# A differential-attention block on one Trainium2 core: GpSimd combines the two softmax maps, and the head's output is scaled only in its norm

## The chip, the core and the metric

The program runs on one core of one Trainium2 chip. The metric is the device time of one execution in microseconds (us). The kernel before takes 1281.97 us, the median of three runs (1281.35 to 1283.07). The engines are named as in the profile: PE is TensorE (matmuls and transposes, with PEld for its weight loads), DVE is VectorE, ACT is ScalarE, POOL is GpSimd and SP is SyncE, which issues most of the DMAs. Each engine works through its own instructions in a fixed order, and a semaphore holds an instruction until what it needs is there.

## The reference

The block is one decoder layer on 1024 tokens of width 1024, in float32. After an RMS norm one projection gives a pooling branch, queries, keys and values, and two gates. What the change touches is the differential attention: four heads, each with two maps of head dimension 64 and a value of width 128.

```python
def probs(qq, kk):
    s = jnp.einsum('bhqd,bhkd->bhqk', qq, kk).astype(jnp.float32) * scale + bias
    s = jnp.where(causal, s, -jnp.inf)
    return jax.nn.softmax(s, axis=-1)

a = probs(qa, k1) - lam * probs(qb, k2)
o = jnp.einsum('bhqk,bhkd->bhqd', a.astype(vh.dtype), vh)
...
o = rms_norm(o, subln_g) * (1.0 - lambda_init)     # per head, over the 128 value columns
```

`rms_norm` divides by the root of the mean square plus 1e-6. Then both branches go through their own projections, are multiplied by their gates, summed, projected, normed and added to the input, and a SwiGLU feed-forward part of hidden width 2816 follows.

## The kernel before

The program has a projection part (units of seven products that save an eighth one, about 0 to 338 us), the attention (about 338 to 500 us), the second branch projection and the output projection, and the feed-forward part. Matrix products are done in pieces: each float32 operand is split by ACT into a rounded high part and by DVE into the remainder, and three matmuls of 512 columns replace one.

The attention works on 32 steps, one for each head h and each block qb of 128 queries. With E = exp(scores), a step needs L = 128 (qb + 1) columns. `scores(h, qb)` makes for each of the two maps m: matmuls into a PSUM pair (L734, L735), one DVE instruction that adds the distance bias, leaves the negated scores in the tile E[m] and their minimum in nm (L738), and one ACT exponential that also sums each row (L741). Then three DVE instructions join the two maps: the reciprocals of both sums, the factor cf = sum0 * nlam / sum1 where nlam is minus lambda, and E0 + cf * E1 (L745 to L747). So the joined map is still too large by the first map's sum. `transposes(h, qb)` turns it on PE in blocks of 128 (L762), and ACT and DVE split it into AT (L764). `values(h, qb)` multiplies by V (L776), and ACT and DVE scale the two halves of the product by 1/sum0 and add them into O (L781, L782); ACT sums the squares (L784). `head_norm(h)` makes one factor per row from these sums (DVE, then a power on POOL, L126) and DVE multiplies the head's O by it (L795); `turn_head` transposes O for the projection (L808 to L811).

The steps of the first three heads go in the order 7, 0, 6, 1, 5, 2, 4, 3 of qb, those of the last in falling order. The code issues the scores of step i + 4, then the transposes of step i + 1, then the values of step i. Between these, `filling()` hands out matmuls of the rest of the last projection unit and of the branch projection `branch(0, ...)` as filler for PE, at a pace given by PACES. Outside the stretches marked as manual, a planner with its own costs then sets the final order on every engine, so a change of an instruction's engine also moves others. `branch(1, ...)` follows the attention in the code; its first two products need only the later half of the queries.

The tiles E and AT share 14 buffers (tag b4) with others, the small columns 20 (tag small); the PSUM has two buffers each for pairs, for mm (transposes and values) and for fil (filler).

Of the kernel before, what the change touches and what calls it, by code (L numbers as in the profile page):

```python
# [39 lines left out]
def block_kernel(ctx, tc, x, w_in, pool_mix, pool_scale, w_branch_a, lam_q1, lam_k1, lam_q2,  # L40
# [72 lines left out]
    make_identity(nc, ident)  # L113
    mhalf = cp.tile([P, 8], F32, name="mhalf")
    nc.vector.memset(mhalf, -0.5)
    junk = cp.tile([P, D], mybir.dt.bfloat16, name="junk")
    psc = cp.tile([P, 4], F32, name="psc")
    sgc = cp.tile([P, 1], F32, name="sgc")
# [596 lines left out]
    def scores(h, qb):  # L715

        QA, QB, K, V = heads[h]
        slope = 0.25 ** (h + 1)
        L = P * (qb + 1)
        nj = 1 if L <= HALF else 2  # L720
        w = L // nj
        q = slice(qb * P, (qb + 1) * P)
        if nj == 1:
            E = b4([P, 2, HALF], F32, "E")
            E = [E[:, 0, :L], E[:, 1, :L]]
        else:
            E = [b4([P, S], F32, "E")[:, :L] for _ in range(2)]
        nm, sums = small(2, "nm"), small(2, "sums")
        dv = negd[:, S - L:S].rearrange("p (j w) -> p j w", j=nj)
        for m in range(2):  # L730
            sc = pair("s")
            for j in range(nj):
                c = slice(j * w, (j + 1) * w)
                nc.tensor.matmul(sc[:, j, :w], QA[:, m, q], K[:, m, c], start=True, stop=False)  # L734
                nc.tensor.matmul(sc[:, j, :w], QB[:, m, q], K[:, m, c], start=False, stop=True)  # L735
            e = E[m].rearrange("p (j w) -> p j w", j=nj)

            nc.vector.tensor_tensor_reduce(out=e, in0=sc[:, :nj, :w], in1=dv, scale=-slope,  # L738
                                           scalar=3.0e38, op0=ALU.add, op1=ALU.min,
                                           accum_out=nm[:, m:m + 1])  # L740
            nc.scalar.activation(E[m], E[m], AF.Exp, bias=nm[:, m:m + 1], scale=-1.0,  # L741
                                 accum_out=sums[:, m:m + 1])
            yield
        rec, cf = small(2, "rec"), small(1, "cf")
        nc.vector.reciprocal(rec, sums)  # L745
        nc.vector.tensor_scalar(cf, sums[:, 0:1], rec[:, 1:2], nlam, op0=ALU.mult, op1=ALU.mult)
        nc.vector.scalar_tensor_tensor(out=E[0], in0=E[1], scalar=cf, in1=E[0], op0=ALU.mult, op1=ALU.add)  # L747
        attends[h, qb] = E[0], rec
        yield

    O = [b4([P, NB, P], F32, "O") for _ in range(NH)]
    oss = [cp.tile([P, NB], F32, name=name("oss")) for _ in range(NH)]

    def transposes(h, qb):
        E, rec = attends[h, qb]
        ats = []
        for b0 in range(0, qb + 1, 4):
            n = min(4, qb + 1 - b0)
# [6 lines left out]
            sub(AT[:, 1, :n * P], pt[:, :n * P], AT[:, 0, :n * P])  # L765
            ats.append(AT)
            yield
        attends[h, qb] = ats, rec

    def values(h, qb):  # L770
        V = heads[h][3]
        ats, rec = attends[h, qb]
        o = mm("o")[:, :2 * P]
        for b in range(qb + 1):
            for j in range(2):
# [2 lines left out]
            if b == 3:  # L778
                yield
        ov = O[h][:, qb, :]  # L780
        nc.scalar.mul(ov, o[:, P:], rec[:, 0:1])  # L781
        nc.vector.scalar_tensor_tensor(out=ov, in0=o[:, :P], scalar=rec[:, 0:1], in1=ov,  # L782
                                       op0=ALU.mult, op1=ALU.add)
        sumsq(ov, oss[h][:, qb:qb + 1])  # L784
        yield

# [1 line left out]

    def head_norm(h, b=slice(0, NB)):
        n = b.stop - b.start  # L790
        r = rstd_of(oss[h][:, b], n, P)

        def scale():
            o = O[h][:, b, :]
            nc.vector.tensor_tensor(out=o, in0=o, in1=r.unsqueeze(2).to_broadcast([P, n, P]), op=ALU.mult)  # L795

        if h < NH - 1:
            defer(LAG, scale)
        else:
            scale()  # L800
# [480 lines left out]
```

## Time and profile before

| | |
|---|---|
| median of three runs | 1281.97 us (1281.35 to 1283.07) |
| the profiled execution's own time | 1280.2 us |
| its span in the trace | 1278.3 us |
| PE, DVE, ACT, POOL busy, share of the span | 97%, 66%, 46%, 10% |
| granted PE clock, mean | 0.999 |
| attention, about | 338 to 500 us |

The span runs from the first to the last instruction of the trace; 1.9 us of the profiled execution's time lie around it. Shares of the whole span average over stages with different limits, so the attention is read by stretches. PE's busy time holds instructions that overlap: a matmul of 512 columns is shown with some 390 ns, while in a stretch without gaps one starts every 222 ns (90 in 20 us). A busy PE can therefore hold gaps that its busy time does not show.

### The profile page before, as it was taken

The page shows a single profiled execution, that of the slowest core. Times are in us where ns is not written, and L with a number is a line of the kernel's source. Part 1 is how long each engine was busy: PE and PEld are TensorE (multiplying, and loading weights), DVE is VectorE, ACT ScalarE, POOL GpSimd, SP SyncE. Part 2 cuts the span into 40 slices and gives each one's busy share as a digit, 9 for nine tenths or more (in the row PEclk, how much of TensorE's full clock was granted, in tenths as well). Part 3 has the DMA queues.
Part 4 walks back from the last instruction along what each step waited for, and adds up shares of the span by engine and source line. Part 5 has one row for each costly group of instructions (what it writes and reads, how often), then busy time and mean ns, then how long its engine had stood idle before and what let it go on. Part 6 is the DMA issues. An engine that isn't in the chain of part 4 may idle for free.

```text
span 1278.3 us, 15840 instructions
## 1 busy us (share of the span) xinstructions
PE 1246.2 (97%) x5952; PEld 1039.0 (81%) x5952; DVE 839.4 (66%) x1307; ACT 583.0 (46%) x1037; POOL 129.5 (10%) x113
## 2 busy tenths in 40 slices
PE   6999999999989999999999999999999999999997
PEld 6988778888778887878878888888888888888886
DVE  6885775534479987755599556456556537965666
ACT  7453344434586764245454333333333334454542
POOL 1000000000101100000102110111111111000221
PEclk9999999999999999999999999999999999999999
DMA  8263346323788312634224233233322368733235
GB/s 279 83 202 117 134 151 216 110 89 107 251 246 222 121 51 76 196 133 156 98 68 140 99 103 95 93 106 124 108 99 91 107 207 293 250 91 98 87 106 205
DMA packets 139788, 179.16 MB, mean 140 GB/s; under 512 B 8000, under 2 KB 94528, under 8 KB 137280
## 3 DMA queue, kind: packets, MB, share of 16 engines
q1 hardware_dynamic: 127776, 146.56, 36.6%
q10 hardware_dynamic: 11936, 31.60, 6.3%
q8 instruction: 46, 0.75, 0.3%
q14 instruction: 30, 0.25, 0.1%
HBM read 124.39 MB, written 53.74 MB: 139 GB/s over the span
## 4 chain that ended last, share of the span: by engine, by line
PE 79%; DVE 7%; ACT 5%; DMA 4%; issue 4%; POOL 1%; ACTq 0%; SPq 0%; DVEq 0%; POOLq 0%
PE Y L241 9%; PE Y L242 9%; PE Y L243 9%; PE X L241 5%; PE X L242 5%; PE X L243 5%; PE Yd L242 3%; PE Yd L243 3%; PE Yd L241 3%; PE Z L242 2%; PE Z L243 2%; PE Z L241 2%; PE o L776 2%; PE wo L934 2%; PE wo L935 2%
## 5 line engine op out<-in xcount | busy, mean ns | idle before, releaser
L162 DVE TENSOR_TENSOR p<-Z,p 128x512 f32<-128x512 f32 x35 | 24.2, 691 | 156.5 <-PE Z L243 156.4
L242 PE MATMUL Y<-A_lo,Wh 128*128 128x512 f32 x296 | 115.7, 391 | 0.3 <-DVE A_lo L87 0.3
L241 PE MATMUL Y<-A_hi,Wh 128*128 128x512 f32 x296 | 115.3, 389 | 0.0
L243 PE MATMUL Y<-A_hi,Wl 128*128 128x512 f32 x296 | 115.2, 389 | 0.0
L241 PE MATMUL Y<-S_hi,Wh 128*128 128x512 f32 x280 | 109.3, 390 | 0.0
L241 PE MATMUL X<-S_hi,Wh 128*128 128x512 f32 x280 | 109.1, 390 | 0.1
L242 PE MATMUL Y<-S_lo,Wh 128*128 128x512 f32 x280 | 109.2, 390 | 0.0
L243 PE MATMUL Y<-S_hi,Wl 128*128 128x512 f32 x280 | 109.1, 390 | 0.0
L243 PE MATMUL X<-S_hi,Wl 128*128 128x512 f32 x280 | 109.0, 389 | 0.0
L242 PE MATMUL X<-S_lo,Wh 128*128 128x512 f32 x280 | 109.0, 389 | 0.0
L202 ACT CAST Wh<-wf_t 128x1024 fp32r<-128x1024 f32 x70 | 72.8, 1053 | 66.9 <-PE X L242 30.4
L87 DVE TENSOR_TENSOR w_op<-wd,w_op 128x512 fp32r<-128x512 f32 x77 | 56.0, 728 | 52.9 <-ACT w_op L166 52.9
L202 ACT CAST Wh<-w_raw 128x1024 fp32r<-128x1024 f32 x72 | 60.6, 843 | 62.4 <-PE Z L242 40.0
L87 DVE TENSOR_TENSOR Wl<-wf_t,Wh 128x1024 fp32r<-128x1024 f32 x70 | 86.5, 1243 | 1.3 <-ACT Wh L202 1.3
L166 ACT CAST w_op<-wd 128x512 fp32r<-128x512 f32 x77 | 47.9, 623 | 79.5 <-PE Yd L243 31.9
L87 DVE TENSOR_TENSOR Wl<-w_raw,Wh 128x1024 fp32r<-128x1024 f32 x72 | 69.4, 964 | 14.7 <-ACT Wh L202 14.7
L242 PE MATMUL Yd<-w_op,s_op 128*128 128x512 f32 x176 | 68.7, 390 | 0.3 <-DVE w_op L87 0.2
L241 PE MATMUL Yd<-w_op,s_op 128*128 128x512 f32 x176 | 68.6, 390 | 0.0
L243 PE MATMUL Yd<-w_op,s_op 128*128 128x512 f32 x176 | 68.3, 389 | 0.0
L162 DVE TENSOR_TENSOR wf_t<-w_raw,wf_t 128x512 f32<-128x512 f32 x70 | 65.6, 938 | 1.0
L242 PEld LDWEIGHTS Y<-A_lo,Wh 128*128 128x128 f32 x296 | 55.6, 188 | 12.0 <-DVE A_lo L87 0.7
L241 PEld LDWEIGHTS Y<-A_hi,Wh 128*128 128x128 f32 x296 | 55.6, 188 | 11.6
(263 smaller groups left out, 3054.5 us busy)
## 6 DMA issues: line engine op xcount, KB each, us to landing
s_raw<-fsd SPq DMA_DIRECT2D x35, 512.0 KB, 3.7
w_raw<-in_w_in_dram SPq DMA_DIRECT2D x32, 512.0 KB, 4.0
w_raw<-in_w_ffn_gate_dram SPq DMA_DIRECT2D x22, 512.0 KB, 3.7
w_raw<-in_w_ffn_up_dram SPq DMA_DIRECT2D x22, 512.0 KB, 3.7
fsd<-fss SPq DMA_DIRECT2D x11, 1024.0 KB, 3.8
wd<-in_w_ffn_down_dram SPq DMA_DIRECT2D x44, 256.0 KB, 5.0
fsd<-F SPq DMA_DIRECT2D x33, 256.0 KB, 2.3
qkd<-qk_st ACTq DMA_DIRECT2D x16, 512.0 KB, 3.7
```

Source lines behind the costliest of these rows:

```text
L87: nc.vector.tensor_tensor(out=o, in0=a, in1=f32(hi), op=ALU.subtract)
L162: nc.vector.tensor_tensor(out=o, in0=a, in1=b, op=op)
L166: nc.scalar.copy(hi, a)
L202: nc.scalar.copy(hi, a)
L241: nc.tensor.matmul(o, ah, bh, start=start, stop=False, skip_group_check=goes_on)
L242: nc.tensor.matmul(o, ah, bl, start=False, stop=False, skip_group_check=goes_on)
L243: nc.tensor.matmul(o, al, bh, start=False, stop=stop, skip_group_check=goes_on)
L776: nc.tensor.matmul(o, ats[b // 4][:, j, b % 4 * P:(b % 4 + 1) * P], V[:, b, :, :], start=b == 0 and j == 0, stop=b == qb and j == 1)
L934: nc.tensor.matmul(o[e], mh[:, k, :], wl, start=False, stop=False)
L935: nc.tensor.matmul(o[e], ml[:, k, :], wh, start=False, stop=k == KD - 1)
```

## The change

Four things are changed.

1. The three joining instructions leave DVE. POOL now makes cf = sum0 * nlam (one column), rec = sum1 to the power -1 (one column, with a constant tile `mone`), multiplies E1 by rec and cf (two per-partition scalars in one instruction), and adds E1 to E0.
2. 1/sum0 is no longer made. ACT copies one half of the value product and DVE adds the other to it, so O stays larger by sum0.
3. The sums of a head are kept in a tile `esum` of their own until the head's norm, and EPS is multiplied by the square of sum0 there. This takes two DVE instructions in place of one in `head_norm`.
4. The constant tile `mone` is set once on DVE.

```diff
--- before.py
+++ after.py
@@ -113,6 +113,8 @@
     make_identity(nc, ident)
     mhalf = cp.tile([P, 8], F32, name="mhalf")
     nc.vector.memset(mhalf, -0.5)
+    mone = cp.tile([P, 1], F32, name="mone")
+    nc.vector.memset(mone, -1.0)
     junk = cp.tile([P, D], mybir.dt.bfloat16, name="junk")
     psc = cp.tile([P, 4], F32, name="psc")
     sgc = cp.tile([P, 1], F32, name="sgc")
@@ -725,7 +727,7 @@
             E = [E[:, 0, :L], E[:, 1, :L]]
         else:
             E = [b4([P, S], F32, "E")[:, :L] for _ in range(2)]
-        nm, sums = small(2, "nm"), small(2, "sums")
+        nm, sums = small(2, "nm"), esum[h][:, qb, :]
         dv = negd[:, S - L:S].rearrange("p (j w) -> p j w", j=nj)
         for m in range(2):
             sc = pair("s")
@@ -741,18 +743,20 @@
             nc.scalar.activation(E[m], E[m], AF.Exp, bias=nm[:, m:m + 1], scale=-1.0,
                                  accum_out=sums[:, m:m + 1])
             yield
-        rec, cf = small(2, "rec"), small(1, "cf")
-        nc.vector.reciprocal(rec, sums)
-        nc.vector.tensor_scalar(cf, sums[:, 0:1], rec[:, 1:2], nlam, op0=ALU.mult, op1=ALU.mult)
-        nc.vector.scalar_tensor_tensor(out=E[0], in0=E[1], scalar=cf, in1=E[0], op0=ALU.mult, op1=ALU.add)
-        attends[h, qb] = E[0], rec
+        cf, rec = small(1, "cf"), small(1, "rec")
+        nc.gpsimd.tensor_tensor(out=cf, in0=sums[:, 0:1], in1=nlam, op=ALU.mult)
+        nc.gpsimd.tensor_tensor(out=rec, in0=sums[:, 1:2], in1=mone, op=ALU.pow)
+        nc.gpsimd.tensor_scalar(E[1], E[1], rec, cf, op0=ALU.mult, op1=ALU.mult)
+        nc.gpsimd.tensor_tensor(out=E[0], in0=E[0], in1=E[1], op=ALU.add)
+        attends[h, qb] = E[0]
         yield
 
+    esum = [cp.tile([P, NB, 2], F32, name=name("esum")) for _ in range(NH)]
     O = [b4([P, NB, P], F32, "O") for _ in range(NH)]
     oss = [cp.tile([P, NB], F32, name=name("oss")) for _ in range(NH)]
 
     def transposes(h, qb):
-        E, rec = attends[h, qb]
+        E = attends[h, qb]
         ats = []
         for b0 in range(0, qb + 1, 4):
             n = min(4, qb + 1 - b0)
@@ -765,11 +769,11 @@
             sub(AT[:, 1, :n * P], pt[:, :n * P], AT[:, 0, :n * P])
             ats.append(AT)
             yield
-        attends[h, qb] = ats, rec
+        attends[h, qb] = ats
 
     def values(h, qb):
         V = heads[h][3]
-        ats, rec = attends[h, qb]
+        ats = attends[h, qb]
         o = mm("o")[:, :2 * P]
         for b in range(qb + 1):
             for j in range(2):
@@ -778,9 +782,8 @@
             if b == 3:
                 yield
         ov = O[h][:, qb, :]
-        nc.scalar.mul(ov, o[:, P:], rec[:, 0:1])
-        nc.vector.scalar_tensor_tensor(out=ov, in0=o[:, :P], scalar=rec[:, 0:1], in1=ov,
-                                       op0=ALU.mult, op1=ALU.add)
+        nc.scalar.copy(ov, o[:, P:])
+        tt(ov, o[:, :P], ov, ALU.add)
         sumsq(ov, oss[h][:, qb:qb + 1])
         yield
 
@@ -788,7 +791,10 @@
 
     def head_norm(h, b=slice(0, NB)):
         n = b.stop - b.start
-        r = rstd_of(oss[h][:, b], n, P)
+        s0, t, r = esum[h][:, b, 0], small(n, "ms"), small(n, "rstd")
+        nc.vector.scalar_tensor_tensor(out=t, in0=s0, scalar=EPS, in1=s0, op0=ALU.mult, op1=ALU.mult)
+        nc.vector.scalar_tensor_tensor(out=t, in0=oss[h][:, b], scalar=1.0 / P, in1=t, op0=ALU.mult, op1=ALU.add)
+        nc.gpsimd.tensor_tensor(out=r, in0=t, in1=mhalf[:, :n], op=ALU.pow)
 
         def scale():
             o = O[h][:, b, :]
```

The planner gives all engines a new order in the attention. Names carry a running number; `E` is a map, `AT` its split transposes, `O` a head's output, `ms` the mean square, `nm` the minimum, `wb_hi` and `wb_lo` the split weights of a branch projection.

DVE at the norm of head 0, before (tiles of head 1 are E_3370 with 256 columns and E_3433 and E_3434 with 768):

```order
L745 RECIPROCAL rec_3386<-sums_3372 128x2
L746 TENSOR_SCALAR cf_3387<-sums_3372,rec_3386,nlam 128x1
L747 SCALAR_TENSOR_TENSOR E_3370<-E_3370,cf_3387 128x256
L782 SCALAR_TENSOR_TENSOR O_2765<-o_3414,rec_3166,O_2765 128x128
L125 TENSOR_SCALAR ms_3429<-oss_2769 128x8
L738 ISA E_3433,nm_3435<-s_3437,negd_2760 128x768
L738 ISA nm_3435 128x1
L738 ISA E_3434,nm_3435<-s_3444,negd_2760 128x768
L738 ISA nm_3435 128x1
L87 TENSOR_TENSOR AT_3458<-aT_3456,AT_3458 128x128
L795 TENSOR_TENSOR O_2765<-O_2765,rstd_3430 128x1024
L745 RECIPROCAL rec_3451<-sums_3436 128x2
```

The same place on DVE now:

```order
L795 SCALAR_TENSOR_TENSOR ms_3435<-esum_2767 128x8
L87 TENSOR_TENSOR AT_3402<-aT_3397,AT_3402 128x512
L87 TENSOR_TENSOR AT_3417<-aT_3412,AT_3417 128x512
L164 TENSOR_TENSOR O_2771<-o_3420,O_2771 128x128
L796 SCALAR_TENSOR_TENSOR ms_3435<-oss_2775,ms_3435 128x8
L740 ISA E_3440,nm_3442<-s_3443,negd_2762 128x768
L740 ISA nm_3442 128x1
L740 ISA E_3441,nm_3442<-s_3450,negd_2762 128x768
L740 ISA nm_3442 128x1
L87 TENSOR_TENSOR AT_3465<-aT_3463,AT_3465 128x128
L801 TENSOR_TENSOR O_2771<-O_2771,rstd_3436 128x1024
L164 TENSOR_TENSOR O_2772<-o_3472,O_2772 128x128
```

The joins are gone. The norm's multiplication (now L801) still stands behind two biases and one split, with the mean square ahead of them.

POOL at the same place, before (all its work around there):

```order
L97 TENSOR_TENSOR wb_lo_3517<-wb_raw_3515,wb_hi_3516 128x512
L97 TENSOR_TENSOR wb_lo_3770<-wb_raw_3768,wb_hi_3769 128x512
L126 TENSOR_TENSOR rstd_3430<-ms_3429,mhalf 128x8
L97 TENSOR_TENSOR wb_lo_4003<-wb_raw_4001,wb_hi_4002 128x512
L126 TENSOR_TENSOR rstd_3870<-ms_3869,mhalf 128x8
L97 TENSOR_TENSOR wb_lo_4237<-wb_raw_4235,wb_hi_4236 128x512
L97 TENSOR_TENSOR wb_lo_4500<-wb_raw_4498,wb_hi_4499 128x512
```

And now:

```order
L747 TENSOR_TENSOR cf_3391<-esum_2768,nlam 128x1
L748 TENSOR_TENSOR rec_3392<-esum_2768,mone 128x1
L749 TENSOR_SCALAR E_3376<-E_3376,rec_3392,cf_3391 128x256
L750 TENSOR_TENSOR E_3376<-E_3376 128x256
L797 TENSOR_TENSOR rstd_3436<-ms_3435,mhalf 128x8
L747 TENSOR_TENSOR cf_3457<-esum_2768,nlam 128x1
L748 TENSOR_TENSOR rec_3458<-esum_2768,mone 128x1
L749 TENSOR_SCALAR E_3441<-E_3441,rec_3458,cf_3457 128x768
L97 TENSOR_TENSOR wb_lo_3776<-wb_raw_3774,wb_hi_3775 128x512
L750 TENSOR_TENSOR E_3440<-E_3440,E_3441 128x768
L747 TENSOR_TENSOR cf_3507<-esum_2768,nlam 128x1
L748 TENSOR_TENSOR rec_3508<-esum_2768,mone 128x1
```

The power of the norm (rstd) now stands between the joins of two steps, and a split of branch weights (wb_lo) between the two halves of one join.

PE at the end of the attention, before (o is the value product, branch the filler, oT the last transposes of O; y2 is the first branch's operand, OT the second's):

```order
L776 MATMUL o_4650<-V_3750,AT_4618 128x256 x4
L776 MATMUL o_4658<-V_3750,AT_4647 128x256 x2
L243 MATMUL branch_4740<-OTh_4526,wb_lo_4734 128x512
L242 MATMUL branch_4763<-OTl_4527,wb_hi_4756 128x512
L243 MATMUL branch_4763<-OTh_4526,wb_lo_4757 128x512
L241 MATMUL branch_4780<-OTh_4377,wb_hi_4733 128x512
L242 MATMUL branch_4780<-OTl_4378,wb_hi_4733 128x512
L243 MATMUL branch_4780<-OTh_4377,wb_lo_4734 128x512
L241 MATMUL branch_4780<-OTh_4377,wb_hi_4733 128x512
L242 MATMUL branch_4780<-OTl_4378,wb_hi_4733 128x512
L243 MATMUL branch_4780<-OTh_4377,wb_lo_4734 128x512
L808 MATMUL oT_4717<-ident,O_2768 128x128 x4
```

And now:

```order
L766 MATMUL aT_4655<-ident,E_4551 128x128
L243 MATMUL branch_4651<-y2h_3012,wb_hi_4508 128x512
L244 MATMUL branch_4651<-y2l_3013,wb_hi_4508 128x512
L245 MATMUL branch_4651<-y2h_3012,wb_lo_4509 128x512
L780 MATMUL o_4660<-V_3757,AT_4628 128x256 x4
L780 MATMUL o_4668<-V_3757,AT_4657 128x256 x2
L243 MATMUL branch_4651<-y2h_3018,wb_hi_4508 128x512
L244 MATMUL branch_4651<-y2l_3019,wb_hi_4508 128x512
L245 MATMUL branch_4651<-y2h_3018,wb_lo_4509 128x512
L243 MATMUL branch_4651<-y2h_3018,wb_hi_4508 128x512
L244 MATMUL branch_4651<-y2l_3019,wb_hi_4508 128x512
L245 MATMUL branch_4651<-y2h_3018,wb_lo_4509 128x512
```

Before, the first branch's matmuls are all done by then, and 21 of the second's stand ahead of the last value product. Now 30 matmuls of the first branch (6 of them are the last rows here) stand between the last value product and the last oT. Up to the last value product the row of PE holds 51 filler matmuls of 512 columns fewer than before (234 against 285, counted from the first score); they come after it.

## The prediction

> **What bounds the kernel now.** I read the page first, then the stretches of the attention, then the groups, the waits and single instructions there.
>
> ```profile
> span 1278.3 us, 15840 instructions
> PE 1246.2 (97%) x5952; PEld 1039.0 (81%) x5952; DVE 839.4 (66%) x1307; ACT 583.0 (46%) x1037; POOL 129.5 (10%) x113
> ```
>
> PE has next to no room over the span and POOL stands nearly idle. The change touches only the attention, so its stretches decide (PE, PEld, DVE, ACT and POOL busy, instructions in brackets, then clock and DMA):
>
> ```profile
> 300.00:320.00 20.00, 20.00 (x90) 16.57 (x89) 8.57 (x11) 8.35 (x12) 0.00 (x0) 1.00 0.17 66
> ...
> 338.00:360.00 22.00, 21.90 (x104) 17.80 (x103) 11.99 (x31) 18.81 (x29) 0.00 (x0) 1.00 1.02 328
> 360.00:380.00 20.00, 16.00 (x96) 12.71 (x95) 16.78 (x45) 15.92 (x38) 1.98 (x1) 1.00 0.79 252
> 380.00:415.00 35.00, 34.77 (x217) 30.59 (x215) 32.55 (x85) 24.09 (x71) 4.41 (x3) 1.00 0.89 224
> 415.00:450.00 35.00, 33.15 (x204) 28.77 (x204) 32.23 (x84) 24.16 (x71) 4.22 (x3) 1.00 0.34 114
> 450.00:490.00 40.00, 39.98 (x256) 35.34 (x254) 35.87 (x86) 26.82 (x73) 2.93 (x2) 1.00 0.19 60
> 490.00:510.00 20.00, 17.95 (x95) 14.16 (x94) 13.82 (x31) 7.99 (x27) 2.01 (x2) 1.00 0.23 68
> ```
>
> From 380 to 490 us DVE is 92% busy (100.65 of 110 us) beside a PE that is nearly always busy. PE visibly stands still for 0.1 + 4.0 + 0.2 + 1.9 + 0.0 + 2.1 = 8.3 us of these 172. That is a lower bound, since overlapping matmuls hide gaps. The other bound counts what PE had to issue:
>
> ```profile
> 338.00:510.00 172.00, 163.74 (x959) 139.37 (x958) 143.25 (x354) 117.78 (x304) 15.55 (x11) 1.00 0.54 162
> ...
> L776 PE MATMUL o<-V,AT 128*128 128x256 f32 x288 | 39.9, 284 | 1.1 <-DVE AT L87 0.6 <-DVE O L782 0.5
> L734 PE MATMUL s<-K,QA 128*128 128x384 f32 (+5 forms) x94 | 33.0, 353 | 3.2 <-DVE nm L738 3.0
> L762 PE MATMUL aT<-ident,E 128*128 128x128 f32 x144 | 23.9, 276 | 1.9 <-DVE O L782 0.9 <-DVE AT L87 0.9
> L808 PE MATMUL oT<-ident,O 128*128 128x128 f32 x32 | 4.9, 275 | 1.3 <-DVE O L795 1.3
> ...
> 380.70 1.43 PE o L776 x12
> ...
> 387.53 0.44 PE aT L762 x4
> ```
>
> The last two rows are from the chain of waits: a value matmul is issued every 0.119 us, a transpose every 0.11. A 512-column matmul takes 20/90 = 0.222 us. Values 288 x 0.119 = 34.3, transposes 176 x 0.11 = 19.4, scores 32.0 (2 maps x 2 matmuls x 4 heads x 4608 columns), and the other 959 - 288 - 188 - 176 = 307 at 0.222 = 68.2. The sum is 153.9, so up to 18 us are lost. PE's direct waits there, and DVE's own largest, name the cause (us in total, times, longest):
>
> ```profile
> DVE rec L745 <- ACT E L741: 14.0, 14, 3.0
> ...
> PE s L734 <- DVE nm L738: 3.0, 5, 1.0
> ...
> PE oT L808 <- DVE O L795: 1.3, 2, 0.9
> ```
>
> PE waits for DVE, and DVE both works too much and stops 14 times with the reciprocal at the head of its queue until an exponential ends. The stretch is bound by PE and DVE together.
>
> **What DVE loses.**
>
> ```profile
> L747 DVE SCALAR_TENSOR_TENSOR E<-E,cf,E 128x1024 f32<-128x1024 f32 (+3 forms) x16 | 17.8, 1113 | 0.0
> L782 DVE SCALAR_TENSOR_TENSOR O<-o,rec,O 128x128 f32<-128x128 f32 x32 | 11.0, 345 | 2.6 <-ACT O L781 2.5
> L747 DVE SCALAR_TENSOR_TENSOR E<-E,cf 128x128 f32<-128x128 f32 (+3 forms) x16 | 8.7, 545 | 0.1
> L746 DVE TENSOR_SCALAR cf<-sums,rec,nlam 128x1 f32<-128x1 f32 x32 | 8.6, 269 | 0.7
> ...
> L745 DVE RECIPROCAL rec<-sums 128x2 f32<-128x2 f32 x32 | 5.2, 162 | 14.6 <-ACT E L741 14.0
> ...
> L87 DVE TENSOR_TENSOR AT<-aT,AT 128x128 fp32r<-128x128 f32 x8 | 2.3, 282 | 0.0
> ```
>
> Joins: 17.8 + 8.7 + 8.6 + 5.2 = 40.3 us. The plain addition into O replaces an instruction of 345 ns; the nearest row, a 128-column PSUM-minus-SBUF, takes 282, so 32 x 0.063 = 2.0 us more. Five extra small instructions in the norms cost about 0.8. DVE keeps 143.3 - 41.5 = 102 us of the 172, and the 14 us of waits leave its queue. ACT's unscaled copy is at most as long as its scaled one; I count nothing for it.
>
> **What POOL gains.** No row shows the scaling by two columns or the small product on POOL, so both are bounded by their neighbours (minimum/median/maximum ns in rows of that form):
>
> ```profile
> L97 POOL TENSOR_TENSOR wb_lo<-wb_raw,wb_hi x8: 1284/1300/2200, 328.3 to 456.6; 128x512 fp32r<-128x512 f32 x8
> ...
> L684 POOL TENSOR_SCALAR_AFFINE_SELECT negd<-negd 128x1024 f32<-128x1024 f32 x1 | 1.0, 1043 | 0.1
> masks.py:199 POOL TENSOR_SCALAR_AFFINE_SELECT ident<-ident 128x128 f32<-128x128 f32 x1 | 0.3, 292 | 0.1
> L1267 POOL MEMSET const-float32-1.0<- 128x1 f32 x1 | 0.1, 99 | 0.0
> L1187 POOL TENSOR_TENSOR frstd<-fms,mhalf x8: 543/550/935, 1244.4 to 1273.1; 128x1 f32<-128x1 f32 x8
> L126 POOL TENSOR_TENSOR rstd<-ms,mhalf 128x8 f32<-128x8 f32 x3 | 4.9, 1646 | 44.2 <-DVE ms L125 44.2
> L1001 POOL TENSOR_TENSOR fss<-fss,F 128x512 f32<-128x512 f32 x11 | 18.1, 1641 | 0.9
> ```
>
> The two selections, with one input, give 751 ns for 896 columns: 0.84 ns a column and 185 ns fixed. With that fixed part, the two-input row costs (1300 - 185)/512 = 2.18 ns a column. A head has 8 joins and 4608 columns:
> - addition: 8 x 0.185 + 4608 x 0.00218 = 11.5 us;
> - scaling: 5.3 us at the selection's rate, 11.5 at the two-input rate. It has one tensor input, so it is nearest to the selection; I take 6.5 for its two column operands;
> - power: 8 x 0.55 = 4.4;
> - small product: between 0.10 (the memset) and 0.55 (the power); I take 0.2, so 1.6;
> - two handovers per join at 0.9/11 = 0.08: 1.3.
>
> This is 25.3 us a head (23.3 to 33.1). With what POOL already does there (a 1.65 power and one or two splits of 1.3) it is 29 (27 to 37), against 35 a head now: room in the middle, none at the upper end.
>
> Elementwise work with two inputs belongs on VectorE by the Trainium skill, GPSIMD Engine Reference, "Engine selection", which calls GpSimd about twice as slow there and roughly line-rate with one input. Rows here agree for two inputs: 1300 against 684 ns. By the 4497 ns for 2048 columns of that page's "Elementwise — side-by-side cycle accounting" the addition would be an estimated 11.1 us a head instead of 11.5.
>
> **Is a join in time?** In head 1 the 768-column step is tightest, behind POOL's power for the norm and beside a split (ACT's last exponential, then PE's first transpose of it):
>
> ```profile
> 399.76 0.93 ACT L741 ACTIVATE E<-E,nm 128x768 f32<-128x768 f32 x1
> ...
> 408.76 0.60 PE L762 MATMUL aT<-ident,E 128*128 128x128 f32 x4
> ```
>
> The sum is read at 400.8, so 8.0 us are left. The join takes 0.2 + 0.55 + 0.16 + 1.0 + 1.86 = 3.8, the power 1.65 and the split 1.3: 6.7, ready 1.3 us early. At the upper bounds the join is 5.0 (product 0.55, scaling 1.86) and ready just in time. Other joins have more.
>
> **What gets a new wait.** DVE's norm multiplication now waits for a power that stands behind a join on POOL, and behind it on DVE stand an addition into O and the next step's biases, for which PE's values and scores wait. It also reads two SBUF tensors while POOL works:
>
> ```profile
> 399.79 1.21 DVE L795 TENSOR_TENSOR O<-O,rstd 128x1024 f32<-128x1024 f32 x1
> ...
> 433.36 1.29 POOL L97 TENSOR_TENSOR wb_lo<-wb_raw,wb_hi 128x512 fp32r<-128x512 f32 x1
> 433.52 2.21 DVE L795 TENSOR_TENSOR O<-O,rstd 128x1024 f32<-128x1024 f32 x1
> ```
>
> It lost 1.0 us when POOL was running. This is the lock that the Trainium skill gives in SBUF — State Buffer, "Who interferes with whom": a DVE instruction with two SBUF inputs and a GpSimd instruction that reads SBUF exclude each other for their whole length; the trace agrees, with 1.0 us. The old join read two SBUF tensors as well, so 32 possible meetings go; three long norm multiplications remain. I charge 0.5 us of PE for each head's norm, 1.5 us.
>
> **The sum.** At the end (490 to 510) 30 first-branch matmuls, 30 x 0.222 = 6.7 us, now lie over the chain of sum, power, scaling and transposes: of 2.05 us idle I give back 1.7. From 415 to 450, where DVE loses about 10 us of 32, 1.4 of 1.85. From 360 to 380, where ACT is 80% busy too, 2.0 of 4.0. Of the hidden 18 - 8 = 10 us a quarter, 2.4. Less 1.5 and 0.5 for joins a little late: 7.5 - 2.0 = 5.5 us. The profiled execution of 1280.2 (span 1278.3 and 1.9 around it) becomes 1274.7; the median of the runs lies 1.8 above it, so the forecast is 1276.5 us.
>
> The 51 filler matmuls that moved behind the last value product (11.3 us) are no gain by themselves: the attention must end 11.3 us sooner only to break even, and the forecast asks for 11.3 + 5.5 - 1.7 = about 15.
>
> **Rivals.**
> - Nothing measurable (1282). What DVE frees is eaten by the norm's waits, 2 us a head instead of 0.5, and by joins 0.5 us late in several steps. For it: the power behind a join. Against: 8 us of slack per join.
> - POOL becomes the bound, slower. It decides when a head's POOL work passes 35 us, that is when the scaling costs more than (35 - 3.6 - 11.5 - 4.4 - 1.6 - 1.3 - 1.5)/4608 = 2.4 ns a column, just over the two-input rate. At twice the two-input rate (a pass for each factor) a head needs 3.6 + 11.5 + 4.4 + 1.6 + 1.3 + 21.6 = 44 us, 9 us late in each of three heads: 1309. Against it: one tensor input. The rule of the Trainium skill named above is this rival in general form.
> - The attention does not shorten although DVE is free, because the chains through ACT (exponential, split, sum of squares) set the pace. Then the moved filler lies behind it: 11.3 us more, less about 6 that come back at the end and in the fuller DVE, 1287. For it: ACT is 86% and 80% busy in the first two stretches (18.81 of 22 and 15.92 of 20); against: 68% from 380 to 490.
> - Nearly all gaps close: 13 of the 18 us, 1269. It needs POOL at the lower bound and no wait at the norms.
>
> **How the numbers follow.** A measurement of this kernel tells a difference of 0.2%, 2.6 us, from none. Chances: the forecast 0.48, all gaps 0.10, nothing 0.21, POOL the bound 0.10, moved filler 0.11. That gives faster 0.57, the same 0.22, slower 0.21 (a little of the forecast's case lies within 0.2%). The forecast's own range is 1273 to 1280. To leave out no more than 2 in 10 it reaches from 1270, most of the gaps closed, to 1287, the moved filler; the 1309 stays outside.
>
> **What would show it.** Right: DVE below 80% from 380 us on with no wait for an exponential in its queue; PE's transposes not waiting for POOL; the last value product some 15 us earlier and the tail without gaps. Wrong: a scaling much over 1.2 us for 1024 columns; long waits of transposes for POOL; the norm multiplication waiting microseconds for its power; a last value product that comes less than 11 us earlier.

## The result, and the profile after

The changed kernel takes 1276.12 us, the median of five runs (1275.54 to 1278.52), the kernel before 1281.35 us beside it (1279.42 to 1283.07). The ratio is 0.9962, with a 95% interval of 0.9947 to 0.9977: 0.4% faster, by the interval 3 to 7 us. The profiled execution of the changed kernel took 1276.9 us.

First the head of the page of the changed kernel (span, then busy time, share and instructions of each engine):

```profile
span 1275.1 us, 15989 instructions
PE 1244.8 (98%) x5952; PEld 1040.9 (82%) x5952; DVE 807.7 (63%) x1217; ACT 579.2 (45%) x1037; POOL 224.8 (18%) x241
```

The stretches of the attention, after the change (length; PE, PEld, DVE, ACT, POOL busy, instructions in brackets; clock, DMA share, GB/s):

```profile
338.00:360.00 22.00, 20.93 (x94) 17.61 (x95) 7.89 (x19) 16.80 (x23) 8.74 (x12) 0.92 1.03 329
360.00:380.00 20.00, 17.42 (x105) 14.24 (x103) 12.44 (x32) 17.57 (x46) 14.38 (x21) 1.00 0.75 234
380.00:415.00 35.00, 34.78 (x227) 31.18 (x225) 25.87 (x68) 25.62 (x82) 30.50 (x39) 1.00 1.03 246
415.00:450.00 35.00, 35.00 (x218) 31.22 (x217) 26.54 (x64) 25.66 (x74) 31.10 (x40) 1.00 0.28 94
450.00:490.00 40.00, 37.80 (x249) 33.17 (x248) 29.94 (x69) 26.14 (x79) 25.37 (x31) 1.00 0.15 47
490.00:510.00 20.00, 20.00 (x92) 16.58 (x91) 11.08 (x17) 3.18 (x5) 0.00 (x0) 1.00 0.45 145
338.00:510.00 172.00, 165.92 (x974) 144.00 (x975) 113.75 (x265) 114.97 (x305) 110.09 (x139) 0.99 0.57 166
```

From 380 to 490 us DVE is busy 82.35 of 110 us (75%), where it was 100.65 (92%). POOL goes from 15.55 us to 110.09 in the 172. PE's visible gaps from 415 to 450 and from 490 to 510 are gone, and 2.2 us of new ones stand between 450 and 490.

POOL's groups in this stretch (line, operation, out<-in, shape, count, busy us, mean ns, idle before):

```profile
L750 POOL TENSOR_TENSOR E<-E,E 128x1024 f32<-128x1024 f32 (+3 forms) x16 | 31.8, 1986 | 1.1
L749 POOL TENSOR_SCALAR E<-E,rec,cf 128x1024 f32<-128x1024 f32 (+7 forms) x32 | 26.4, 824 | 3.3
L748 POOL TENSOR_TENSOR rec<-esum,mone 128x1 f32<-128x1 f32 x32 | 18.6, 582 | 12.4 <-ACT E L743 9.4 <-DVE ma L164 1.7 <-PE s L737 0.7
L750 POOL TENSOR_TENSOR E<-E 128x128 f32<-128x128 f32 (+3 forms) x16 | 14.0, 878 | 1.3
L97 POOL TENSOR_TENSOR wb_lo<-wb_raw,wb_hi 128x512 fp32r<-128x512 f32 x6 | 7.8, 1297 | 0.4 <-ACT wb_hi L95 0.4
L747 POOL TENSOR_TENSOR cf<-esum,nlam 128x1 f32<-128x1 f32 x32 | 7.1, 220 | 18.2 <-ACT E L743 18.2
L797 POOL TENSOR_TENSOR rstd<-ms,mhalf 128x8 f32<-128x8 f32 (+1 forms) x5 | 7.0, 1399 | 7.3 <-DVE ms L796 5.7 <-DVE ms L795 1.4
```

The sum is 112.7 us (the rows overlap a little, so it lies 2.6 us above POOL's busy time), and 5.7 us more of idle time ahead of scalings and additions, the handovers: 29.6 us a head. The largest and the smallest scaling, from the same view with shapes kept apart:

```profile
L749 POOL TENSOR_SCALAR E<-E,rec,cf 128x1024 f32<-128x1024 f32 x4 | 4.8, 1199 | 0.4
...
L749 POOL TENSOR_SCALAR E<-E,rec,cf 128x128 f32<-128x128 f32 x4 | 1.8, 448 | 0.4
```

The waits that matter (us in total, times, longest). No exponential is waited for in DVE's queue any more; POOL waits for them instead. DVE's idle time now stands mostly ahead of the splits that ACT has to round first (20.0 us, 1.4 before). PE and its weight loads wait for POOL's E 0.5 us in all, and DVE's norm multiplication (L801) for its power 1.8:

```profile
DVE AT L87 <- ACT AT L768: 20.0, 18, 6.0
...
POOL cf L747 <- ACT E L743: 18.2, 5, 11.1
...
POOL rec L748 <- ACT E L743: 9.4, 9, 3.7
...
DVE O L801 <- POOL rstd L797: 1.8, 3, 1.1
...
PEld aT L766 <- POOL E L749: 0.5, 1, 0.5
```

The wait for the norm's power was there before the change as well:

```profile
DVE O L795 <- POOL rstd L126: 1.6, 2, 1.1
```

Last, the value products and the first group of the output projection: after the change, and in a second profile of the kernel before, taken later (the row gives ns, then the first and last start).

```profile
L780 PE MATMUL o<-V,AT x288: 274/283/386, 365.7 to 485.5; 128*128 128x256 f32 x144
...
L939 PE MATMUL wo<-woh,mh x128: 387/389/499, 536.4 to 632.4; 128*128 128x512 f32 x128
```

```profile
L776 PE MATMUL o<-V,AT x288: 274/283/386, 365.9 to 500.7; 128*128 128x256 f32 x144
...
L933 PE MATMUL wo<-woh,mh x128: 387/389/497, 541.9 to 637.9; 128*128 128x512 f32 x128
```

The last value product comes 15.2 us earlier; about 11.3 of these are the filler that now lies behind it (51 matmuls at 0.222); the output projection begins 5.5 us earlier, and the spans differ by 1280.3 - 1275.1 = 5.2. In the first profile of before the last value product stood at 497.9, only 12.4 us later than now: that execution had a luckier start (the last experiment).

### The profile page after: what moved, and what is told of

It is laid out like the page before. It is cut to its first block, busy times and chain, and to the rows that moved or that the text cites. A ratio compares the mean times of both kernels' runs of the same rounds, so it can differ in the third digit from the quotient of the medians.

```text
span 1275.1 us, 15989 instructions
## 1 busy us (share of the span) xinstructions
PE 1244.8 (98%) x5952; PEld 1040.9 (82%) x5952; DVE 807.7 (63%) x1217; ACT 579.2 (45%) x1037; POOL 224.8 (18%) x241
## 4 chain that ended last, share of the span: by engine, by line
PE 85%; DVE 6%; ACT 3%; DMA 2%; issue 2%; POOL 1%; ACTq 0%; SPq 0%; DVEq 0%; POOLq 0%
PE Y L243 10%; PE Y L244 10%; PE Y L245 10%; PE X L243 5%; PE X L244 5%; PE X L245 5%; PE Yd L244 3%; PE Yd L245 3%; PE Yd L243 3%; PE Z L244 2%; PE Z L245 2%; PE Z L243 2%; PE o L780 2%; PE branch L245 2%; PE branch L243 2%
## 5 line engine op out<-in xcount | busy, mean ns | idle before, releaser
L243 PEld LDWEIGHTS Y<-A_hi,Wh 128*128 128x128 f32 x296 | 55.6, 188 | 11.5
```

Source lines behind the costliest of these rows:

```text
L243: nc.tensor.matmul(o, ah, bh, start=start, stop=False, skip_group_check=goes_on)
```

## The experiments

Times are medians; each ratio is to the kernel before, run on the same chip beside it (1281.0 to 1282.0 us).

**The two halves of the change.** The first kernel moves the join alone: the power makes both reciprocals, and outputs and norm are as before.

```diff
+        nc.gpsimd.tensor_tensor(out=rec, in0=sums, in1=mone, op=ALU.pow)      # two columns
...
+        nc.scalar.mul(ov, o[:, P:], rec[:, 0:1])       # and the old scaled addition, the old head_norm
```

> Only the join is moved to GpSimd; the outputs are still scaled by 1/sum0 in ACT and DVE and the head norm is the old one (the power on GpSimd makes both reciprocals, two columns in place of one). DVE still loses the 40.3 us of the joins, not the 2.0 us of the plain addition. Theory A (the join's leaving DVE is the gain): most of it stays, 1276.5 to 1278 (ratio to before 0.996 to 0.9975). Theory B (the shorter output chain through ACT and DVE is at least half of the gain): 1278.5 to 1281 (0.998 to 1.0).

The second leaves the join on DVE and takes only the unscaled outputs and the new norm.

```diff
-        nc.gpsimd.tensor_tensor(out=cf, ...)      # and the other three instructions of the join
+        nc.vector.reciprocal(rec, sums[:, 1:2])
+        nc.vector.tensor_scalar(cf, sums[:, 0:1], rec, nlam, op0=ALU.mult, op1=ALU.mult)
+        nc.vector.scalar_tensor_tensor(out=E[0], in0=E[1], scalar=cf, in1=E[0], op0=ALU.mult, op1=ALU.add)
```

> Only the outputs stay unscaled and the head norm takes the square of the sum; the join stays on DVE in three instructions (one-column reciprocal, factor, product and addition). DVE loses only 2.0 us of 143 and still waits for the exponentials. Theory A: nothing measurable, 1280 to 1282 (0.999 to 1.0005). Theory B (the output chain is at least half of the gain): 1278.5 or less (0.998 or less). The planner puts 18 of the filler matmuls behind the last value product here.

Measured: the join alone 1278.15 us, ratio 0.9969 (0.9956 to 0.9981); the outputs alone 1280.98, 0.9988 (0.9979 to 0.9998). The two losses of time, 0.31% and 0.12%, add up to the whole change's 0.38% within their intervals. Most of the gain is the join's, as theory A had it; its 1278.15 us lie 0.15 above A's range, its ratio inside. The outputs give at most a small part of their own, 1.5 us by the ratio and 0.7 by the medians, by the ratio a little more than A allowed. Theory B falls. Both kernels also have a new order on every engine, and an order alone can cost about 3 us (the kernel with twelve matmuls moved, below), so this small part is not certain.

**Is the deferred filler a gain by itself?** The kernel before with a slower filler pace alone leaves 49 branch matmuls behind the last value product, and the changed kernel with a faster pace has as many ahead of it as the kernel before.

```diff
-PACES = (2.2, 0.5, 0.3, 0.3)
+PACES = (2.2, 0.5, 0.25, 0.25)      # in the kernel before; 0.4, 0.4 in the changed kernel
```

> The kernel before with a slower filler pace alone (0.25 for 0.3), which leaves 49 of the branch matmuls behind the last value product, about as many as the change does (51). Theory A (the deferral is no gain of its own: while DVE binds, the attention cannot end 11 us sooner, so a part of the 10.9 us comes on top, less some cover at the tail): 1282 to 1288 (1.0005 to 1.005). Theory C (the gain of the change is the new order with its filler at the tail): 1276 to 1278 (0.996 to 0.998).

> The changed kernel with a faster filler pace (0.4 for 0.3), so that 211 branch matmuls lie before the last value product, as in the kernel before (213), and not 162. Theory A (about 2 us of the gain is the tail covered by the deferred filler): 1277 to 1279 (0.997 to 0.9985). Theory C (the deferral is the gain): 1281 or more. Theory D (the deferral costs, since PE starves between 360 and 490 us where filler was taken out): 1271 to 1275 (0.9925 to 0.995).

Measured: 1290.82 us for the first, 1.0064 (1.0051 to 1.0077), above even theory A's range, and 1277.38 for the second, 0.9966 (0.9954 to 0.9978). The old join with less filler between, by stretches:

```profile
380.00:415.00 35.00, 33.22 (x203) 28.69 (x202) 31.17 (x81) 22.82 (x67) 2.94 (x2) 1.00 0.73 183
415.00:450.00 35.00, 33.29 (x204) 28.50 (x203) 31.98 (x82) 24.57 (x71) 5.52 (x4) 1.00 0.38 125
450.00:490.00 40.00, 35.64 (x230) 29.64 (x229) 36.46 (x88) 28.18 (x77) 3.00 (x2) 1.00 0.11 34
```

DVE is as busy as before (99.6 of 110 us), and PE now shows the gaps that filler had covered (7.9 us). Its last value product starts at 496.5, 1.4 to 4.2 us sooner than in the two profiles of before, though 10.9 us of matmuls had been taken out, and the kernel lost 9 us. So the attention was held by more than PE's work, and moving its filler behind it costs nearly its whole length. With the join on POOL both placings give the same time within the intervals (1276.1 and 1277.4): the attention then shrinks as filler is taken out. With about as much filler behind the last value product, the kernel before takes 1290.8 us and the changed one 1276.1. That difference, 13 to 15 us by ratios or medians, is far more than a new order costs (about 3 us, below). The tail's cover is worth about a microsecond there, and theories C and D fall.

**DVE's work or DVE's waits?** The change took 40 us of work from DVE and 14 us of waits at the head of its queue. This kernel gives the work back without a wait.

```diff
+        nc.vector.tensor_reduce(out=junk2[:, 0:1], in_=negd[:, :L], axis=mybir.AxisListType.X, op=ALU.max)
+        nc.vector.tensor_reduce(out=junk2[:, 1:2], in_=negd[:, :HALF], axis=mybir.AxisListType.X, op=ALU.max)
         attends[h, qb] = E[0]
```

> The changed kernel with work on DVE that nothing waits for and that waits for nothing: after each join two maxima over constant columns (as many as the map has, and 512), whose results are not used. By the old join's 1113 ns for 1024 columns and 545 for smaller ones they take about 40 us in all, as much as the change took from DVE, and read one SBUF tensor, not two. Theory P (DVE's busy time was what bound): the gain is lost, 1280 to 1284 (0.999 to 1.002). Theory Q (the 14 us in which the reciprocal at the head of DVE's queue waited for an exponential were it): the gain stays, 1275 to 1278 (0.995 to 0.9975).

Measured: 1280.50 us, 0.9996 (0.9986 to 1.0005), the gain is gone. Its groups on DVE and two stretches:

```profile
L752 DVE TENSOR_REDUCE junk<-negd 128x1 f32<-128x896 f32 (+7 forms) x30 | 22.3, 742 | 0.0
L753 DVE TENSOR_REDUCE junk<-negd 128x1 f32<-128x512 f32 x30 | 20.3, 676 | 0.0
```

```profile
360.00:380.00 20.00, 15.16 (x87) 12.72 (x86) 19.72 (x44) 15.10 (x36) 12.56 (x17) 0.91 0.70 227
380.00:415.00 35.00, 33.62 (x212) 29.54 (x211) 33.77 (x77) 25.21 (x78) 30.21 (x38) 1.00 0.93 226
```

42.6 us of work that nothing reads bring DVE to 99% and 96% in these stretches and the time back to that of before. The largest loss that shows is from 360 to 380 us: PE's gaps there grow from 2.6 us in the changed kernel to 4.8, its clock is 0.91, and up to 380 us its transposes wait 3.5 us for DVE's splits (0.3 in the whole attention of the changed kernel). So DVE's work is enough to hold PE up. It is not shown that the work alone made the old loss. From 338 to 510 us DVE is busy 146.5 us, 3 to 5 more than in the two profiles of before, so a share of the old waits for exponentials is not excluded. The planner also moved some instructions for the added work (about 140 of 5952 on PE), and a new order alone can cost about 3 us, as the kernel with twelve matmuls moved shows below; so a large part of the 4 us could be the order's.

**How much room has POOL?** Without the scaling, POOL has 8 us a head less to do.

```diff
-        nc.gpsimd.tensor_scalar(E[1], E[1], rec, cf, op0=ALU.mult, op1=ALU.mult)
```

> The changed kernel without the scaling on GpSimd: it adds the two maps unscaled, so the joined map is not the reference's; the order on all other engines is the same. GpSimd loses 6.6 us a head (its busy share of the attention falls from 0.7 to 0.5). Theory A (joins are in time, only one step or two is tight): 1274.5 to 1277 (0.9945 to 0.9965). Theory E (GpSimd paces the attention, or its joins are late often): 1265 to 1272 (0.987 to 0.9925).

Measured: 1275.71 us, 0.9953 (0.9941 to 0.9965). The interval overlaps that of the change, and the order on PE, ACT and DVE is the same: POOL does not set the change's time. Then the other way, the scaling in two passes, each by one column:

```diff
-        nc.gpsimd.tensor_scalar(E[1], E[1], rec, cf, op0=ALU.mult, op1=ALU.mult)
+        nc.gpsimd.tensor_scalar(E[1], E[1], rec, None, op0=ALU.mult)
+        nc.gpsimd.tensor_scalar(E[1], E[1], cf, None, op0=ALU.mult)
```

> The changed kernel, with the scaling on GpSimd in two passes (by rec, then by cf) in place of one; the order on every other engine is the same. A pass of a head took 6.6 us, so GpSimd needs 25.9 + 3.3 + 6.6 = 36 us a head, where a head of the attention takes (485.5 - 339) / 4 = 37. Theory A with the forecast's threshold of 35 us: joins come about 1 us late in three heads, 1277 to 1281 (ratio to before 0.9965 to 0.9995). Theory E (GpSimd paces the attention already): 6.6 us more in each of three heads, 1290 to 1296 (1.007 to 1.011). Theory F (a join has far more slack than that): no change, 1275 to 1277 (0.995 to 0.9965).

Measured: 1345.38 us, 1.0498 (1.0485 to 1.0512), far outside every theory, because the price I put on a pass was wrong. POOL's rows of this kernel:

```profile
L749 POOL TENSOR_SCALAR E<-E,rec 128x1024 f32<-128x1024 f32 x4 | 11.4, 2859 | 0.4
...
L749 POOL TENSOR_SCALAR E<-E,rec 128x128 f32<-128x128 f32 x4 | 2.5, 614 | 0.2
```

A pass with one multiplication takes 2859 ns where the change's pass with two takes 1199. Two more kernels separate the form from the second pass: two passes with two columns each (one of them ones), and one pass with one column, the factor being multiplied first.

```diff
+        nc.gpsimd.tensor_scalar(E[1], E[1], rec, one, op0=ALU.mult, op1=ALU.mult)    # the first kernel
+        nc.gpsimd.tensor_scalar(E[1], E[1], cf, one, op0=ALU.mult, op1=ALU.mult)
...
+        nc.gpsimd.tensor_tensor(out=cf, in0=cf, in1=rec, op=ALU.mult)                # the second kernel
+        nc.gpsimd.tensor_scalar(E[1], E[1], cf, None, op0=ALU.mult)
```

> The changed kernel with the scaling in two passes again, but each pass with two column operands as in the change (rec and a column of ones, cf and the ones). In the run with passes by one column each took 2859 ns for 1024 columns, where the change's pass by two columns takes 1199. Theory G (the form with a single column is the slow one): a pass takes 1.2 us here, GpSimd needs 25.9 + 3.3 + 6.6 + 0.8 = 36.6 us a head, as long as a head lasts (36.6), so 1276 to 1282 (ratio to before 0.996 to 1.0005). Theory H (a second pass over the same tile is slow in any form, by its dependence on the first): 2.8 us a pass and about 1345 (1.05).

> The changed kernel with the factor multiplied first (one more one-column product, 0.2 us) and then one pass by this single column, the plainest way to write the join; the order on all other engines is the same. Theory G (the form with a single column costs 2859 ns for 1024 columns, 13.9 us a head, against 6.6): GpSimd needs 25.9 + 3.3 + 7.3 + 2.2 = 38.7 us a head, about 2 us more than a head lasts, in each of four heads and with some slack before it: 1277 to 1290 (0.997 to 1.007). If the form is not slow by itself: 1275 to 1278 (0.995 to 0.9975), with passes of 1.2 us.

Measured: 1295.26 us, 1.0104 (1.0088 to 1.0120), and 1304.03, 1.0158 (1.0143 to 1.0173). The scaling in the first and in the second:

```profile
L751 POOL TENSOR_SCALAR E<-E,rec,one 128x1024 f32<-128x1024 f32 x4 | 4.8, 1206 | 0.4
```

```profile
L750 POOL TENSOR_SCALAR E<-E,cf 128x1024 f32<-128x1024 f32 x4 | 11.4, 2857 | 0.4
```

Theory G holds for the price: the form with a single column is slow, in one pass as in two. Both times lie above what I expected, so POOL's limit lies lower than the 35 us a head of the forecast. With POOL's rows of a head added up as above (busy time and handovers; the time is the median minus that of before):

| kernel | POOL, us a head | time against before, us |
|---|---|---|
| no scaling | 21.7 | -5.3 |
| the change | 29.6 | -5.2 |
| two passes of two columns | 37.0 | +13.3 |
| one pass of one column | 39.3 | +22.1 |
| two passes of one column | 51.5 | +64.4 |

The last three are 18.5, 27.3 and 69.6 us above the change. If all four heads pay their full excess, that is 4.6, 6.8 and 17.4 us a head, and POOL begins to decide at an estimated 32.4, 32.5 and 34.1 us a head. The trace agrees: in the changed kernel the power of POOL's first join starts at 347.2 and its last addition at 478.7 us, 132 us with its length, or 33 a head. So I take that span, and not the whole length of the attention, for what POOL has; it rests on this agreement. The change uses 90% of it. The wait that shows where POOL is late (the three slow kernels in the order of the table, then their stretch from 415 to 450):

```profile
DVE O L804 <- POOL rstd L800: 13.0, 5, 4.6
```

```profile
DVE O L802 <- POOL rstd L798: 16.9, 5, 6.2
```

```profile
DVE O L802 <- POOL rstd L798: 19.1, 5, 7.9
...
PE aT L767 <- POOL E L751: 20.6, 7, 5.8
```

```profile
415.00:450.00 35.00, 31.26 (x190) 27.45 (x189) 21.78 (x56) 21.58 (x66) 33.26 (x42) 0.95 0.33 104
```

```profile
415.00:450.00 35.00, 29.70 (x181) 25.74 (x180) 20.73 (x52) 20.07 (x62) 33.00 (x40) 0.92 0.33 101
```

```profile
415.00:450.00 35.00, 28.99 (x151) 24.92 (x150) 19.69 (x51) 21.19 (x64) 33.63 (x29) 0.85 0.44 122
```

The norm multiplication waits at the head of DVE's queue for a power that stands behind joins; PE's transposes wait for POOL's E 20.6 us in the last kernel, but only 2.0 and 0.4 in the other two. POOL is busy 94 to 96% of the stretch, and most of the rest is handovers.

**The start of the attention.** PE waits there for the first head's QB load. Two kernels tried to take that wait away: one sent the three weight loads ahead of it in SyncE's queue through GpSimd, the other had twelve more matmuls of the last projection unit issued first.

```diff
-                ws[d] = load_w(w[:, d * P:(d + 1) * P], 4, P, "wb", e == 0)
+                ws[d] = load_w(w[:, d * P:(d + 1) * P], 4, P, "wb", e == 0, nc.gpsimd if e == 0 and d < 3 else None)
...
-    for _ in range(4):       # the second kernel
+    for _ in range(8):
         next(last_unit)
```

> The changed kernel, with the first three weight loads of the first branch projection issued by GpSimd in place of SyncE; in SyncE's queue the first head's QB load stood behind them, and the order of everything else is the same. In the profiles so far PE waited 1.0 to 2.75 us for QB at about 336 us, and in some the granted clock was low for 3 us behind it (1.4 us lost). If the wait goes: 1272 to 1275 (0.9925 to 0.995). If another load is late instead (V, the next head's, or the weights themselves): 1275 to 1278 (0.995 to 0.9975).

> The changed kernel with twelve more matmuls of the last projection unit (2.7 us) issued ahead of the first scores, so that PE has work while the first head's QB load is under way; the weight loads were not what held that load back, its buffer was. In nine profiles PE waited 1.0 to 2.75 us there, and in most the granted clock fell for 3 us behind the wait (8 matmuls at 0.43 us in place of 0.22: 1.5 us). If both go: 1271.5 to 1274.5 (0.9925 to 0.995). If the attention merely starts later and ends later, since its chains set its length: 1275 to 1278 (0.995 to 0.9975).

Measured: 1276.42 us, 0.9961 (0.9949 to 0.9974), and 1279.50, 0.9985 (0.9974 to 0.9996). The waits stayed, 2.6 and 2.5 us. In the first kernel SyncE had nothing else ahead of the load, and issued it no earlier than before:

```profile
331.45 3.06 SPq L667 DMA_DIRECT2D QB<-qkd  x4
```

```profile
SPq L667 <- PE Y L245: 36.1, 1, 36.1
```

So it is not the queue that holds it: the second row, of the waits of SyncE's queue, shows it standing 36.1 us at this load until a matmul of PE had ended. That fits a buffer that PE still reads, but no run here freed it sooner. In the second kernel the planner put the twelve matmuls ahead of the first score product and left the one that needs QB at the same place in PE's order (the 1631st of PE's in both); the edit did not do what it was made for. It is still 3.4 us slower than the change, outside both expectations. Its work is the same; what differs is the order, with 83 of 5952 instructions on PE, 77 of 1037 on ACT and 30 of 1217 on DVE out of their old sequence. Which of them costs the time stays open, but a difference of about 3 us between two kernels with different orders can be the order's alone. Last, the kernel before was profiled again.

> The kernel before, unchanged, for a second profile of its start. Its first profile has a wait of 1.04 us for QB and no low clock behind it; the changed kernel and its variants 1.85 to 2.75 us. If that differs from run to run: a wait near 2 us here. If the change causes it: 1.0 us again.

```profile
338.27 0.47 PE L735 MATMUL s<-K,QB 128*128 128x512 f32 x1 [2.67 <-DMA QB<-qkd]
...
339.82 0.63 PE L241 MATMUL Z<-A_hi,Wh 128*128 128x512 f32 x1
340.25 0.63 PE L242 MATMUL Z<-A_lo,Wh 128*128 128x512 f32 x1
```

One time, 1282.13 us. Its wait is 2.67 us and the low clock follows: the wait differs from one execution to the next and is not the change's doing. Compared with this profile the change's trace shows the 5.2 us that the medians show.

## Why the prediction was right, point by point

- **The time.** 1276.5 was forecast, 1276.12 measured. The sum was 5.5 us; the medians differ by 5.2, and the output projection starts 5.5 us earlier when profiles with a like start are compared. The profiled execution, forecast at 1274.7, took 1276.9. Its wait for QB was 2.7 us, where the profile that the forecast started from had 1.0; the kernel before, profiled again with a wait of 2.7, took 1.9 us more too.
- **What bounded.** That the join on DVE holds the attention beside PE is shown: moving it alone gives most of the gain, and with the filler deferred in both kernels the change is worth 13 to 15 us. The prediction named DVE's work and its 14 waits together. The run with useless work shows that work is enough to hold PE up; how the old loss splits into work and waits stays open.
- **What DVE loses.** This term was too large. I took 41.5 us from its 143.3 and expected 102; it is 113.75. The additions into O came as forecast (289 ns in place of 345), but rows were subtracted as if they were busy time. DVE's instructions overlap a little: all its rows of the stretch add up to 163.6 us before and 126.7 after, a fall of 36.9, while its busy time fell by 29.5. The two short norm instructions cost 4.9 us in all, 4.1 more than the one they replace, where 0.8 was added; three of them were held up by POOL (last section). DVE below 80% from 380 us on held all the same: 75%.
- **What POOL gains.** Forecast a head: addition 11.5, scaling 6.5, power 4.4, product 1.6, handovers 1.3, together 25.3. Measured: (31.8 + 14.0)/4 = 11.45, 6.6, 4.65, 1.8 and 1.4, together 25.9. The selection was the right row for the scaling, but only for its form with two columns. With one column it costs (2859 - 614)/896 = 2.5 ns a column, and the change would have been a loss of 22 us. The range of 5.3 to 11.5 us did not hold that form (13.9).
- **The page's rule.** The Trainium skill, GPSIMD Engine Reference, "Engine selection", calls GpSimd roughly line-rate with one input. The trace agrees for the pass with two multiplications (0.84 ns a column) and not for the pass with one (2.5). Its advice to keep two-input elementwise work on VectorE is true for the instruction (2407 ns here for 1024 columns, where DVE's one instruction for product and addition took 1276) and not for this kernel, where DVE's time was short and POOL's was free.
- **Joins in time.** Right: PE's weight loads for the transposes wait 0.5 us for POOL's E, and no other join shows in PE's waits by more than 0.3 us.
- **The new wait.** This term was too large: DVE waits 1.8 us for the power in three waits, but it waited 1.6 in two before, so what is new is 0.2, where 1.5 us of PE were charged. The lock did not lengthen the norm multiplications, whose longest is 1.2 us now; what got longer are short instructions on both engines (last section).
- **The gaps.** At the end 2.1 us were given back, 1.7 forecast; from 415 to 450 all 1.8, 1.4 forecast; from 360 to 380 only 1.4, 2.0 forecast. A new 2.2 us opened from 450 to 490, where after the change less filler is left; the sum had no term for it. Visible gaps fell from 8.5 (second profile of before) to 6.1, that is by 2.5 us. The other 2.7 of the 5.2 are what is left for the hidden gaps, for which 2.4 was taken; no view shows them. So the total is right partly by luck: the visible terms came 2.6 us short of the 5.1 forecast, and the 2.0 charged for waits and late joins made up for most of that, though little of it shows in the trace.
- **The moved filler.** That it is no gain by itself, and that about 15 us are needed: right. The attention ended 15.2 us earlier, which rules out the rival of 1287; the deferral alone, with the join still on DVE, cost the old kernel 9 us.
- **The other rivals.** Nothing measurable falls by the interval. The case that nearly all gaps close (1269) was missed by 7 us.
- **POOL as the bound.** As a mechanism right, as a threshold too high: 32 to 34 us a head, not 35, if POOL has only the time from the first join to the last, 33 us a head. Its price was too low as well if all four heads pay it and not three: for the 44 us of that rival an estimated (44 - 33) x 4 = 44 us and not 27. By this estimate the change passed with about 3 us a head to spare.

## What to carry to other kernels

Work that leaves a crowded engine pays by the time that this engine holds others up. A run that gives the same work back with nothing waiting for it helps to tell the work from the waits, but only if the order of the rest stays as it was: here a new order alone cost 3 us. The room on the engine that takes the work over was here about the time from its first to its last instruction in that stage, not the stage's length, and an instruction that stands behind the moved work in its queue (here the norm's power) was late first. Before GpSimd is given a pass, the exact form has to be timed: the same product with one multiplication or two differed by a factor of 2.4 here.

## What the runs showed of the hardware that was not expected

- **One multiplication is slower than two on GpSimd.** 1024 columns of float32 take 2859 ns with one per-partition column and 1199 ns with two, 128 columns 614 and 448. It was so in three kernels (2859 and 2848 in the first, 2857 in the second, 1206 and 1212 with a column of ones). Why is not known.
- **PE's clock falls behind a stop and where PE starves.** Behind the QB wait, matmuls of 512 columns start 0.43 us apart instead of 0.22 for some 3 us:

```profile
339.07 0.77 PE L737 MATMUL s<-K,QB 128*128 128x512 f32 x1 [2.75 <-DMA QB<-qkd]
...
340.49 0.63 PE L243 MATMUL Y<-S_hi,Wh 128*128 128x512 f32 x1
340.92 0.63 PE L244 MATMUL Y<-S_lo,Wh 128*128 128x512 f32 x1
...
342.07 0.40 PE L244 MATMUL Z<-A_lo,Wh 128*128 128x512 f32 x1
```

  In the three kernels that POOL bounds, the granted clock from 415 to 450 is 0.95, 0.92 and 0.85. The Trainium skill, TensorE: Matmul & The Clock Gate, "Wait — 56ns, not 53.3ns?", gives 426.7 ns for 512 columns on a cold array; the spacing here agrees. In the fourteen profiles of this study that wait is 1.0 to 3.8 us, and in eleven of them such a phase follows before 344 us; it did not after the shortest wait, one of 1.9 and one of 2.4 us, so the length of the stop alone does not decide it.
- **DVE and GpSimd held each other up.** The norm's two instructions over eight columns read SBUF alone. Three of the six took 0.17 to 0.19 us, two of them beside a scaling on POOL. The other three took 0.70, 1.46 and 1.65, and each of these ended within 0.03 us of the end of a two-input addition on POOL that had started before it. It also went the other way: the small product on POOL, 0.19 us as a rule, took 1.12 us where it started behind a norm multiplication on DVE, and ended 0.05 us after it. One pair of each kind, from the two engines' timelines:

```profile
455.10 1.83 POOL L750 TENSOR_TENSOR E<-E,E 128x768 f32<-128x768 f32 x1
...
455.31 1.65 DVE L795 SCALAR_TENSOR_TENSOR ms<-esum 128x8 f32<-128x8 f32 x1
...
397.23 1.21 DVE L801 TENSOR_TENSOR O<-O,rstd 128x1024 f32<-128x1024 f32 x1
...
397.37 1.12 POOL L747 TENSOR_TENSOR cf<-esum,nlam 128x1 f32<-128x1 f32 x1 [0.28 <-ACT E L743]
```

  It fits the exclusion of the two engines that the prediction cites. Two inputs on DVE are not the whole condition: with the join alone moved, the old norm instruction, which reads one tensor, took 1.30 us once, beside an addition on POOL, and 0.17 and 0.32 the other times. No run took POOL's work away from these instructions alone, so the cause is argued from the times, not isolated.
